# A hybrid encoder trunk on one core: the gated-delta stage woven from three generators, with TensorE's order written out

## The chip, the cores and the metric

One core of one Trainium2 chip runs the whole program. The metric is the device time of one execution in microseconds (us); the time of a kernel is the median of its runs.

## The reference

Two layers act on 768 tokens (one sequence of 512, one of 256; width 1024). The change lies in the first layer, in two of its parallel branches:

```
z = h @ w_in
# gated delta rule, 8 heads, chunks of tokens, forward and backward
qkv  = silu(centred_depthwise_conv(z_qkv, gdn_conv_w))        # width 5
q, k = l2_normalize(q) * 128**-0.5, l2_normalize(k)
g    = cumsum(log decay within a chunk);  decay = exp(g_i - g_j), lower part
a    = strict_lower((beta k) k^T * decay)
t_inv = inverse(I + a);  u = t_inv (beta v);  w = t_inv (beta k exp(g))
per chunk, in sequence: v_new = u - w S
                        o     = (q exp(g)) S + (q k^T * decay) v_new
                        S     = S * exp(g_last) + (k exp(g_last - g))^T v_new
y_b  = rms_norm(o_fwd + o_bwd) * silu(g_gdn)
# long convolution: its projections, short convolutions (width 3) and gates
uc = centred_depthwise_conv(z_hy, hy_conv_w) + hy_conv_b;  x0, x1, v = split(uc)
y_a = x0 * bidir_long_conv(v * x1) * silu(g_hy)
```

## The kernel before

The program is written with a tile framework: Python emits instructions, each engine gets its own queue, the framework places the semaphores. Unless told otherwise, a list scheduler orders each engine's queue: among what is ready by its own reckoning, the earliest in program order goes first; weight loads (`wload`) are moved 400 instructions ahead. On the chip each queue runs in that order.

**Projections.** `proj` multiplies one 128-column slice of the weights with all 768 tokens: 8 slices of the contraction, each with three products (high*high, high*low, low*high) over 512 and 256 columns, so 6 matmuls for each slice and 48 for a projection. The result takes one of two PSUM tiles `pp`. A weight slice comes by a DMA of SP's queue (L247), is rounded on ACT (L240), and its low part is made on POOL (L241). In the stage there are 64 projections: for each of 8 heads q, k, v and a gate (`gdn_proj`), for each of 8 channel groups four of the long convolution (`hy_proj`). Behind each come a convolution (`conv`: one ACT pass, L448, then on DVE, L455, eight multiply-adds for the delta rule's, four for the other's) or a gate (`silu2`, L327 on ACT, L328 on DVE).

**A head's front** (`gdn_front`, `gdn_inv`): transposes, norms, the masks `E` (ACT and POOL, L481), the products `A` and `Pm` (L554, L558); then the *gather*, by which the 32x32 diagonal blocks of `A` go through memory (bt to bd, L572; bd to B and W, L573 and L575); then the *inverse* of those blocks, 30 steps of two DVE instructions, each needing the one before (L589, L591); then the *scatter* of the blocks through memory into `TTN` (L592, L596, sixteen DMAs of L602).

**A head's back** (`gdn_back`): two levels of small matmuls that complete the inverse (L618 to L644; L618 is the first reader of `TTN`), the recurrence over chunks in four sequences (matmuls L667 and L668 on the state, L678 with the inverse, L686 and L688), then the norm and the output (`out`, L705 to L719).

The order of the program text is a string at the top:

```
ORDER = "F0 X0 F1 U0 B0 X1 F2 U1 B1 X2 F3 U2 B2 X3 F4 U3 B3 X4 F5 U4 B4 X5 F6 U5 B5 F7 X6 B6 U6 B7 X7 U7"
```

F is a head's projections, front and inverse, B a head's back, X and U are halves of a channel group's projections. So head i+1's projections and front stand before head i's back. The last head's output is emitted inside the next stage, the long convolution (`hyconv`), behind `hy_fwd(0)`.

Of the kernel before, what the change touches and what calls it, by code (L numbers as in the profile page):

```python
# [223 lines left out]
ORDER = "F0 X0 F1 U0 B0 X1 F2 U1 B1 X2 F3 U2 B2 X3 F4 U3 B3 X4 F5 U4 B4 X5 F6 U5 B5 F7 X6 B6 U6 B7 X7 U7"  # L224


class K:
# [34 lines left out]
    def proj(self, whl, m0=0):  # L262
        ps = self.pp.tile([128, 1024], F32, tag="pp", name="pp")[:, :T]
        for k in range(8):
            self.mm3(ps, whl, m0, self.hhi[k], self.hlo[k], k, k == 0, k == 7, ((0, 512), (512, 768)))
        return ps
# [177 lines left out]
    def conv(self, out, ps, taps, tile_ix, width, bias=None):  # L444
# [40 lines left out]
    def gdn_proj(self, p, h, n0):  # L485
        we = self.a["we"]
        kq = p.tile([128, 2, T], F32, tag="kq", name="kq", bufs=2)
        for i, nm in enumerate(("q", "k", "v")):
            w = self.wload(we[n0 + i], self.wp, 128)
            ps = self.proj(w)  # L490
            acc = p.tile([128, T], F32, tag="cv", name="cv", bufs=2)
            self.conv(acc, ps, V_GCW, 8 * i + h, 5)
            if nm == "v":
                vT = p.tile([128, T], F32, tag="vt", name="vT")
                dst = vT
# [4 lines left out]
        ps = self.proj(w)  # L500
        sg = p.tile([128, T], F32, tag="sg", name="sg", bufs=2)
        self.silu2(p, sg, ps)
        return kq, vT, sg

    def gdn_front(self, p, h, E, kq, vT, sg):
# [71 lines left out]
        return dict(kq=kq, sg=sg, kt=kt, nv=nv, rs=rs, ed=ed, A=A, Pm=Pm)  # L577

    def gdn_inv(self, p, h):
# [6 lines left out]
        for m in range(1, 31):  # L586
# [4 lines left out]
            nc.vector.tensor_tensor(out=W[:, :m, m + 1:], in0=W[:, :m, m + 1:], in1=tmp, op=ALU.add)  # L591
        nc.scalar.activation(out=B, in_=W.rearrange("p a b -> p b a"), func=AF.Copy)  # L592
# [11 lines left out]
    def gdn_back(self, p, h, kq, sg, kt, nv, rs, ed, A, Pm):  # L604
# [33 lines left out]
        nc.vector.tensor_scalar_mul(x, tv(ps, 64), -1.0)  # L638
        ps = self.bank()
# [3 lines left out]
        for d, eq, lq in hf:  # L643
            nc.scalar.activation(out=tt[d][eq, :, lq], in_=tv(ps, 64)[eq], func=AF.Copy)  # L644
        yield
# [11 lines left out]
        for step in range(4):  # L657
            for si, (d, seq) in enumerate(seqs):
                if step >= len(seq):
                    continue  # L660
                t = seq[step]
                ts = slice(128 * t, 128 * t + 128)
                if step == 0:
                    v1 = nv[:, t, :]
                else:
                    ps = self.bank()
                    mm(ps[:, :128], kq[:, 0, ts], S[si])  # L667
                    mm(ps[:, 128:256], kq[:, 1, ts], S[si])  # L668
                    v1 = p.tile([128, 128], F32, tag="v1", name="v1", bufs=3)
                    nc.vector.scalar_tensor_tensor(out=v1, in0=ps[:, :128], scalar=self.gneg[:, d, t, h:h + 1], in1=nv[:, t, :], op0=ALU.mult, op1=ALU.add)  # L670
                    eg = self.gex[:, 3 * d, t, h:h + 1]
                    if t not in seen:
                        nc.scalar.activation(out=o[:, t, :], in_=ps[:, 128:256], func=AF.Copy, scale=eg)
                        seen.add(t)
                    else:
                        nc.vector.scalar_tensor_tensor(out=o[:, t, :], in0=ps[:, 128:256], scalar=eg, in1=o[:, t, :], op0=ALU.mult, op1=ALU.add)
                ps = self.bank()
                mm(ps[:, :128], TTN[:, d, t, 0:128], v1)  # L678
                w = p.tile([128, 128], F32, tag="wv", name="wv", bufs=2)
                nc.vector.tensor_copy(w, ps[:, :128])  # L680
                last = step == len(seq) - 1
                if not last:
                    w2 = p.tile([128, 128], F32, tag="w2", name="w2", bufs=2)
                    nc.scalar.activation(out=w2, in_=ps[:, :128], func=AF.Copy, scale=ed[:, d, t:t + 1])
                ps = self.bank()
                mm(ps[:, :128], Pm[:, d, t, :], w)  # L686
                if not last:
                    mm(ps[:, 128:256], kt[:, t, :], w2)  # L688
# [12 lines left out]
                yield  # L701

# [9 lines left out]
        y = sg  # L712
        for t0, n in ((0, 4), (4, 2)):
# [4 lines left out]
            nc.vector.scalar_tensor_tensor(out=y[:, cs], in0=pt[:, :128 * n], scalar=self.vec(V_GN), in1=sg[:, cs], op0=ALU.mult, op1=ALU.mult)  # L718
        nc.scalar.dma_start(out=self.y[8 + h], in_=y)  # L719


    def hy_proj(self, p, c, n0, halves=(0, 1)):
        nc = self.nc

        def part(i):
            w = self.wload(self.a["we"][n0 + i], self.wp, 128)
            ps = self.proj(w)
            t = p.tile([128, T], F32, tag="hy", name="hy", bufs=2)
            if i < 3:
                self.conv(t, ps, V_HCW, 8 * i + c, 3, bias=self.vec(V_HCB + 8 * i + c))  # L730
            else:
                self.silu2(p, t, ps)
            return t
        for i, j, dst in [((1, 2, self.ud[c]), (0, 3, self.xd[c]))[x] for x in halves]:
            t0, t1 = part(i), part(j)
            nc.gpsimd.tensor_tensor(out=t1, in0=t1, in1=t0, op=ALU.mult)
            nc.scalar.dma_start(out=dst, in_=t1)

# [611 lines left out]
def trunk(tc, a, outs, dbg=None):  # L1350
    nc = tc.nc
    dbg = dbg or {}
    with ExitStack() as ctx:
# [24 lines left out]
        with ExitStack() as gd:  # L1378
# [32 lines left out]
            def front(i):  # L1411
                if i > 0:
# [151 lines left out]
```

## Time and profile before

| what | value |
|---|---|
| median of 3 runs | 2365.88 us (2364.73 to 2366.44) |
| the profiled execution | 2362.44 us, of which the span from first to last instruction is 2360.7 us |
| TensorE (PE) busy over the span | 2213.2 us (94%) |
| VectorE (DVE) / ScalarE (ACT) / GpSimd (POOL) busy | 1414.8 / 896.5 / 433.9 us |
| mean granted clock of TensorE | 0.974 of full speed |
| the stage of the change | 222.2 to 1044.2 us of the span |

Busy time counts instructions at work; a share of the span is a mean over stages with different limits, so the stage is looked at by itself.

### The profile page before, as it was taken

The numbers are of one execution on the slowest core, as the hardware profiler recorded it, in microseconds if no ns is written. First come the engines' busy times: TensorE is split into PE (matmuls) and PEld (weight loads), VectorE is DVE, ScalarE is ACT, GpSimd is POOL, SyncE is SP. The second block draws the span as 40 slices with busy tenths as digits, with TensorE's granted clock in tenths as the row PEclk, the third lists the DMA queues.
The fourth block names the chain that finished last, engine by engine and source line by source line (L and its number), as shares of the span: only waits on it lengthen the run. The fifth ranks groups of instructions, "written<-read, shape, count | busy, mean of one in ns | idle before, by whom it ended". The sixth has DMA issues, their size and how long they took to land. (4 is left out here: it accounts for less than half of the span.)

```text
span 2360.7 us, 35185 instructions
## 1 busy us (share of the span) xinstructions
PE 2213.2 (94%) x13648; PEld 1855.1 (79%) x13648; DVE 1414.8 (60%) x3236; ACT 896.5 (38%) x1888; POOL 433.9 (18%) x303
## 2 busy tenths in 40 slices
PE   8999898889999998889999979999999999999897
PEld 6788776777878887777778858988888877778785
DVE  6775387785776867758651264236555577664414
ACT  6333544435345344322142352122222344443423
POOL 2344242223233231223300140000000000000002
PEclk9999999999999998999999989999999999999898
DMA  7442223222223222246362342111111211111613
GB/s 247 138 158 96 73 84 78 82 82 73 78 73 90 78 62 60 67 165 222 113 197 62 102 135 90 54 56 58 52 46 43 77 50 50 40 62 46 203 63 107
DMA packets 122705, 218.98 MB, mean 93 GB/s; under 512 B 49592, under 2 KB 62297, under 8 KB 122282
## 3 DMA queue, kind: packets, MB, share of 16 engines
q1 hardware_dynamic: 102746, 171.86, 23.9%
q10 hardware_dynamic: 19568, 44.04, 5.0%
q8 instruction: 107, 1.75, 0.3%
q0 software_dynamic: 224, 0.83, 0.1%
q14 instruction: 60, 0.49, 0.1%
HBM read 174.43 MB, written 42.25 MB: 92 GB/s over the span
## 5 line engine op out<-in xcount | busy, mean ns | idle before, releaser
L256 PE MATMUL pp<-hhi,w 128*128 128x512 f32 (+1 forms) x2032 | 558.5, 348 | 20.5 <-DVE cv L455 9.6
L258 PE MATMUL pp<-hlo,w 128*128 128x512 f32 (+1 forms) x2032 | 553.6, 347 | 0.0
L260 PE MATMUL pp<-hhi,w 128*128 128x512 f32 (+1 forms) x2032 | 545.9, 344 | 0.0
L256 PEld LDWEIGHTS pp<-hhi,w 128*128 128x128 f32 (+1 forms) x2032 | 321.2, 190 | 68.3 <-issue 17.2
L258 PEld LDWEIGHTS pp<-hlo,w 128*128 128x128 f32 (+1 forms) x2032 | 319.4, 190 | 47.9 <-issue 6.6
L260 PEld LDWEIGHTS pp<-hhi,w 128*128 128x128 f32 (+1 forms) x2032 | 318.0, 189 | 44.8 <-issue 2.7
L1013 PE MATMUL pp<-yh,wo 128*128 128x256 f32 (+1 forms) x1152 | 274.1, 348 | 17.3 <-DVE wo L241 9.0
L240 ACT ACTIVATE w<-wr 128x1024 fp32r<-128x1024 f32 x155 | 163.3, 1053 | 296.6 <-PE pp L260 247.3
L241 POOL TENSOR_TENSOR w<-wr,w 128x1024 fp32r<-128x1024 f32 (+1 forms) x65 | 155.3, 2389 | 462.5 <-ACT w L240 305.4
L1013 PEld LDWEIGHTS pp<-yh,wo 128*128 128x128 f32 x1152 | 191.5, 195 | 48.8 <-ACT yh L240 11.5
L241 DVE TENSOR_TENSOR w<-wr,w 128x1024 fp32r<-128x1024 f32 x90 | 113.6, 1263 | 140.3 <-ACT w L240 140.1
L241 DVE TENSOR_TENSOR wo<-wor,wo 128x640 fp32r<-128x640 f32 (+1 forms) x76 | 62.0, 817 | 191.5 <-ACT wo L240 191.4
L1013 PE MATMUL pp<-yl,wo 128*128 128x512 f32 (+1 forms) x576 | 170.2, 349 | 0.2
L241 POOL TENSOR_TENSOR xk<-raw,xk 128x512 fp32r<-128x512 f32 x8 | 10.8, 1356 | 751.7 <-ACT xk L240 751.7
L455 DVE SCALAR_TENSOR_TENSOR cv<-pp,vecs,cv 128x510 f32<-128x510 f32 (+1 forms) x192 | 107.4, 605 | 24.7 <-ACT cv L448 24.7
L1013 PEld LDWEIGHTS pp<-yl,wo 128*128 128x128 f32 x576 | 100.1, 194 | 17.3 <-DVE yl L241 1.9
L240 ACT ACTIVATE wo<-wor 128x640 fp32r<-128x640 f32 (+1 forms) x76 | 52.0, 686 | 159.1 <-PE pp L1013 146.4
L589 DVE TENSOR_TENSOR Bt<-W,B 48x30 f32<-48x30 f32 (+14 forms) x240 | 98.5, 410 | 4.2 <-DMA B<-bd 2.5
L591 DVE TENSOR_TENSOR W<-W,Bt 48x30 f32<-48x30 f32 (+14 forms) x240 | 97.9, 408 | 1.8
L1022 POOL TENSOR_TENSOR oacc<-oacc,osq 128x768 f32<-128x768 f32 (+2 forms) x15 | 24.0, 1601 | 279.6 <-ACT osq L1018 279.6
L455 DVE SCALAR_TENSOR_TENSOR hy<-pp,vecs,hy 128x511 f32<-128x511 f32 x96 | 55.6, 606 | 30.6 <-ACT hy L448 30.2
L686 PE MATMUL pb<-wv,P 128*128 128x128 f32 x192 | 42.4, 303 | 20.9 <-DVE wv L680 20.9
(322 smaller groups left out, 3736.4 us busy)
## 6 DMA issues: line engine op xcount, KB each, us to landing
wr<-we SPq DMA_DIRECT2D x72, 512.0 KB, 3.5
wr<-wog SPq DMA_DIRECT2D x30, 512.0 KB, 3.6
wor<-weo SPq DMA_DIRECT2D x40, 320.0 KB, 3.2
wr<-wqk SPq DMA_DIRECT2D x24, 512.0 KB, 3.3
wor<-woo SPq DMA_DIRECT2D x36, 256.0 KB, 3.0
yr<-ye SPq DMA_DIRECT2D x20, 384.0 KB, 3.9
dec<-dec ACTq DMA_DIRECT2D x8, 768.0 KB, 4.3
fd<-F ACTq DMA_DIRECT2D x8, 768.0 KB, 3.5
```

Of the source, the lines that this page charges most:

```text
L240: nc.scalar.activation(out=hi, in_=src, func=AF.Copy)
L241: (lo_eng or self.lo_eng or nc.vector).tensor_tensor(out=lo, in0=src, in1=hi.bitcast(F32), op=ALU.subtract)
L256: mm(ps[:, s:e], wh, rhs_hi[:, s:e], start=first, stop=False)
L258: mm(ps[:, s:e], wh, rhs_lo[:, s:e], start=False, stop=False)
L260: mm(ps[:, s:e], wl, rhs_hi[:, s:e], start=False, stop=last)
L455: nc.vector.scalar_tensor_tensor(out=out[:, lo:hi], in0=ps[:, lo + s:hi + s], scalar=self.vec(taps + 24 * j + tile_ix), in1=out[:, lo:hi], ...
L589: nc.vector.tensor_tensor(out=tmp, in0=W[:, :m, m:m + 1].to_broadcast([48, m, n]), in1=B[:, m:m + 1, m + 1:].to_broadcast([48, m, n]), op= ...
L591: nc.vector.tensor_tensor(out=W[:, :m, m + 1:], in0=W[:, :m, m + 1:], in1=tmp, op=ALU.add)
L686: mm(ps[:, :128], Pm[:, d, t, :], w)
L1013: mm(ps[:, s:e], w[:, wi, j, :], y[order[i], g], start=i == 0 and x == 0, stop=i == nk - 1 and x == 2)
L1022: nc.gpsimd.tensor_tensor(out=acc[:, s:e], in0=acc[:, s:e], in1=sq[:, s:e], op=ALU.add)
```

## The change

The stage becomes three generators that are advanced in turns. A *piece* is six matmuls of a projection (one slice of the contraction). For every piece of `big` (all projections: per head four of the delta rule and then 24 pieces, three projections, of the long convolution) the loop advances the pending convolutions and gates (`k.post`) by four steps, the recurrences (`sb`) by one and the fronts (`sf`) by one. Inside this block TensorE's queue is not scheduled: it is in program order. The other engines are scheduled as before. A head's front is followed by ten empty pieces before its back may start; a front may start when the head two before it is done. The last head's output is now emitted inside the block. In the recurrence the sequences of a step are emitted side by side (all L667 and L668, then all L678, then all L686 and L688). `kq` has three buffers instead of two, `v1`, `wv` and `w2` four.

In steps of one piece, a front has 4 for the transposes of k and q, 2 for those of v, 6 empty ones, 3 for the products (L554), 30 for the inverse and the 10 empty ones behind it; the gather's instructions stand at the inverse's first step, the scatter's behind its last. A back has 9 for the two levels, then 8, 12, 9 and 9 for the recurrence's four steps (step 1 has four sequences, the last two steps have two), 4 empty ones and 2 for the output's transposes. `hy_proj` is cut into pieces and posts in the same way as `gdn_proj`.

```diff
-ORDER = "F0 X0 F1 U0 B0 X1 F2 U1 B1 ..."
+    def proj_g(self, whl):
+        ps = self.pp.tile([128, 1024], F32, tag="pp", name="pp")[:, :T]
+        for k in range(8):
+            self.mm3(ps, whl, 0, self.hhi[k], self.hlo[k], k, k == 0, k == 7, ((0, 512), (512, 768)))
+            if k < 7:
+                yield
         return ps
-    def conv(self, out, ps, taps, tile_ix, width, bias=None):
+    def conv_g(self, out, ps, taps, tile_ix, width, bias=None):
...
                 nc.vector.scalar_tensor_tensor(
...
+                yield
-    def gdn_proj(self, p, h, n0):
+    def gdn_proj(self, p, h, n0, settled):
...
+        for i, nm in enumerate(("q", "k", "v")):
+            w = self.wload(we[n0 + i], self.wp, 128)
+            ps = yield from self.proj_g(w)
+            self.post.append(post(i, nm, ps))
+            yield
         w = self.wload(we[n0 + 3], self.wp, 128)
+        ps = yield from self.proj_g(w)
+        settled()
+        self.post.append(post_g(ps))
+        yield
+        return st
@@ gdn_front
+            yield
+        for _ in range(6):
+            yield
...
@@ gdn_inv
             nc.vector.tensor_tensor(out=W[:, :m, m + 1:], in0=W[:, :m, m + 1:], in1=tmp, op=ALU.add)
+            yield
...
@@ gdn_back
-            for si, (d, seq) in enumerate(seqs):
...
+            live = [(si, d, seq[step], step == len(seq) - 1) for si, (d, seq) in enumerate(seqs) if step < len(seq)]
+            v1s, ws = {}, {}
+            for si, d, t, last in live:
...
+                yield
+            if 0 < len(live) < 4 and step:
+                yield
+            for si, d, t, last in live:
...
+                ws[si] = w, w2
+                yield
+            if len(live) < 4:
+                yield
+            for si, d, t, last in live:
+                w, w2 = ws[si]
...
                 yield
+            if len(live) < 4:
+                yield
...
+        for _ in range(4):
+            yield
...
-    def hy_proj(self, p, c, n0, halves=(0, 1)):
+    def hy_proj(self, p, c, n0):
...
-            for ch in ORDER.split():
...
+            def small_front():
+                for i in range(8):
+                    while i not in fronts or i - 2 in st:
+                        yield
+                    E, q = fronts.pop(i)
+                    sg = q.pop("sg")
+                    st[i] = dict((yield from k.gdn_front(p, i, E, **q)), sg=sg)
+                    yield from k.gdn_inv(p, i)
+                    for _ in range(10):
+                        yield
+                    backs.append(i)
+            def small_back():
+                for i in range(8):
+                    while i not in backs:
+                        yield
+                    yield from k.gdn_back(p, i, **st[i])
+                    del st[i]
+            def big():
+                hys = chain(*(k.hy_proj(p, c, 32 + 4 * c) for c in range(8)))
+                for i in range(8):
+                    if i > 0:
+                        E = k.gdn_decay(p, i)
+                    q = yield from k.gdn_proj(p, i, 4 * i, lambda: settled(i - 2))
+                    if i == 0:
+                        k.gdn_gates(p)
+                        E = k.gdn_decay(p, 0)
+                    while "sg" not in q:
+                        run(k.post)
+                    fronts[i] = E, q
+                    for _ in range(24):
+                        next(hys)
+                        yield
+                yield from hys
...
+            with tc.manual_schedule(engines={mybir.EngineType.PE}):
+                for _ in big():
+                    for _ in range(4):
+                        run(k.post)
+                    next(sb, None)
+                    next(sf, None)
+                while k.post:
+                    run(k.post)
+                for _ in sb:
+                    next(sf, None)
...
                     f = k.hy_fwd(p2, 0)
-                out(7)
```

## Rows read from the trace of the kernel before

**Rows 1.** Busy time by stretch: length, then PE, PEld, DVE, ACT, POOL, clock, DMA.

```profile
222.20:1044.20 822.00, 750.04 (x5560) 640.15 (x5559) 572.74 (x1608) 360.56 (x909) 230.53 (x108) 0.97 0.27 79
662.40:758.60 96.20, 89.71 (x688) 77.24 (x687) 70.24 (x200) 44.63 (x112) 28.85 (x13) 1.00 0.28 79
674.60:709.70 35.10, 31.81 (x210) 28.00 (x209) 34.00 (x107) 11.45 (x33) 6.85 (x3) 1.00 0.13 43
```

**Rows 2.** Waits of PE in the stage: us in total, times, longest.

```profile
PE pb L686 <- DVE wv L680: 20.9, 18, 2.5
...
PE pb L426 <- DVE g L423: 4.2, 1, 4.2
...
PE pb L332 <- ACT zT L404: 1.9, 1, 1.9
```

**Rows 3.** Timeline of PE: start, us, engine, line, operation, tiles, shape.

```profile
660.19 0.51 PE L256 MATMUL pp<-hhi,w 128*128 128x512 f32 x2
...
661.25 0.51 PE L256 MATMUL pp<-hhi,w 128*128 128x512 f32 x2
...
678.78 0.39 PE L667 MATMUL pb<-S,kq 128*128 128x128 f32 x2
679.00 0.39 PE L668 MATMUL pb<-S,kq 128*128 128x128 f32 x2
```

**Rows 4.** Timeline of DVE: end of a gather's input, an inverse's first and last.

```profile
655.93 1.08 DVE L558 TENSOR_TENSOR A<-pb,A 128x256 f32<-128x256 f32 x3 [1.51 <-POOL A L539]
...
674.62 0.14 DVE L589 TENSOR_TENSOR Bt<-W,B 48x30 f32<-48x30 f32 x1
...
682.13 2.52 DVE L591 TENSOR_TENSOR W<-W,Bt 48x210 f32<-48x210 f32 x1
...
709.51 0.20 DVE L591 TENSOR_TENSOR W<-W,Bt 48x30 f32<-48x30 f32 x1
```

**Rows 5.** Timeline of SP's queue, the DMAs of gather and scatter.

```profile
660.51 2.00 SPq L572 DMA_DIRECT2D bd<-bt  x4
...
668.90 0.33 SPq L573 DMA_DIRECT2D B<-bd  x1
...
718.69 3.02 SPq L602 DMA_DIRECT2D TTN<-wd  x6
```

**Rows 6.** DMA issues, 500 to 900 us: count, KB each, median us to landing.

```profile
TTN<-wd SPq DMA_DIRECT2D x64, 24.0 KB, 2.4
...
bd<-bt SPq DMA_DIRECT2D x16, 48.0 KB, 2.5
```

**Rows 7.** Groups of DVE in one inverse, 674.6 to 709.7: busy us, mean ns | idle.

```profile
L591 DVE TENSOR_TENSOR W<-W,Bt 48x30 f32<-48x30 f32 (+14 forms) x30 | 13.0, 433 | 0.3
L589 DVE TENSOR_TENSOR Bt<-W,B 48x30 f32<-48x30 f32 (+14 forms) x30 | 11.3, 378 | 0.2
...
L455 DVE SCALAR_TENSOR_TENSOR hy<-pp,vecs,hy 128x511 f32<-128x511 f32 (+1 forms) x4 | 2.4, 599 | 0.0
```

**Rows 8.** Groups of DVE in the stretch behind it, 709.8 to 758.6.

```profile
L455 DVE SCALAR_TENSOR_TENSOR cv<-pp,vecs,cv 128x510 f32<-128x510 f32 (+3 forms) x24 | 13.3, 608 | 1.9 <-ACT cv L448 1.9
...
L328 DVE SCALAR_TENSOR_TENSOR kq<-th,cv 128x768 f32<-128x768 f32 x2 | 1.9, 954 | 1.0 <-ACT th L327 1.0
```

**Rows 9.** Timeline of POOL: two masks, and a weight's low part.

```profile
658.22 3.98 POOL L481 TENSOR_TENSOR E<-E,cm 128x768 f32<-128x768 f32 x2
...
682.02 2.40 POOL L241 TENSOR_TENSOR w<-wr,w 128x1024 fp32r<-128x1024 f32 x1 [11.10 <-ACT w L240]
```

**Rows 10.** Timeline of PE where the stage ends.

```profile
1039.95 0.82 PE L332 MATMUL pb<-cm,eu 128*128 128x128 f32 x6
...
1043.96 1.06 PE L826 MATMUL pb<-Rf,f 128*128 128x128 f32 x8
1046.44 0.63 PE L332 MATMUL pb<-cm,o 128*128 128x128 f32 x4 [1.42 <-DVE o L711]
...
1051.03 1.22 PE L905 MATMUL pp<-g,Y 128*128 128x257 f32 x2 [2.91 <-POOL Y L879]
```

More of the change, by code (lines that the diff above doesn't have):

```diff
@@ L483, in gdn_decay, with post @@
         return E
-    def gdn_proj(self, p, h, n0):
+    def gdn_proj(self, p, h, n0, settled):
         we = self.a["we"]
[L487 to L490, printed above, removed]
+        st = {}
+        kq = st["kq"] = p.tile([128, 2, T], F32, tag="kq", name="kq", bufs=3)
+        def post(i, nm, ps):
             acc = p.tile([128, T], F32, tag="cv", name="cv", bufs=2)
-            self.conv(acc, ps, V_GCW, 8 * i + h, 5)
+            yield from self.conv_g(acc, ps, V_GCW, 8 * i + h, 5)
             if nm == "v":
-                vT = p.tile([128, T], F32, tag="vt", name="vT")
-                dst = vT
+                dst = st["vT"] = p.tile([128, T], F32, tag="vt", name="vT")
             else:
@@ new lines, in gdn_back @@
+                    v1s[si] = nv[:, t, :]
+                    continue
+                ps = self.bank()
+                mm(ps[:, :128], kq[:, 0, ts], S[si])
+                mm(ps[:, 128:256], kq[:, 1, ts], S[si])
+                v1 = v1s[si] = p.tile([128, 128], F32, tag="v1", name="v1", bufs=4)
+                nc.vector.scalar_tensor_tensor(out=v1, in0=ps[:, :128], scalar=self.gneg[:, d, t, h:h + 1], in1=nv[:, t, :], op0=ALU.mult, op1=ALU.add)
+                eg = self.gex[:, 3 * d, t, h:h + 1]
@@ L677, in gdn_back @@
+                if t not in seen:
+                    nc.scalar.activation(out=o[:, t, :], in_=ps[:, 128:256], func=AF.Copy, scale=eg)
+                    seen.add(t)
+                else:
+                    nc.vector.scalar_tensor_tensor(out=o[:, t, :], in0=ps[:, 128:256], scalar=eg, in1=o[:, t, :], op0=ALU.mult, op1=ALU.add)
+                yield
+            if 0 < len(live) < 4 and step:
+                yield
+            for si, d, t, last in live:
                 ps = self.bank()
-                mm(ps[:, :128], TTN[:, d, t, 0:128], v1)
@@ L679, in gdn_back @@
-                w = p.tile([128, 128], F32, tag="wv", name="wv", bufs=2)
+                mm(ps[:, :128], TTN[:, d, t, 0:128], v1s[si])
+                w = p.tile([128, 128], F32, tag="wv", name="wv", bufs=4)
                 nc.vector.tensor_copy(w, ps[:, :128])
-                last = step == len(seq) - 1
+                w2 = None
                 if not last:
-                    w2 = p.tile([128, 128], F32, tag="w2", name="w2", bufs=2)
+                    w2 = p.tile([128, 128], F32, tag="w2", name="w2", bufs=4)
@@ L684, in gdn_back @@
                     nc.scalar.activation(out=w2, in_=ps[:, :128], func=AF.Copy, scale=ed[:, d, t:t + 1])
+                ws[si] = w, w2
+                yield
+            if len(live) < 4:
+                yield
+            for si, d, t, last in live:
+                w, w2 = ws[si]
                 ps = self.bank()
+                if not last:
+                    mm(ps[:, 128:256], kt[:, t, :], w2)
                 mm(ps[:, :128], Pm[:, d, t, :], w)
                 if not last:
-                    mm(ps[:, 128:256], kt[:, t, :], w2)
@@ L701, in gdn_back @@
                 yield
+            if len(live) < 4:
+                yield
         self.mark("g.out%d" % h)
@@ L712, in gdn_back @@
         y = sg
+        for _ in range(4):
+            yield
         for t0, n in ((0, 4), (4, 2)):
@@ L718, in gdn_back, with post, gate @@
             nc.vector.scalar_tensor_tensor(out=y[:, cs], in0=pt[:, :128 * n], scalar=self.vec(V_GN), in1=sg[:, cs], op0=ALU.mult, op1=ALU.mult)
+            yield
         nc.scalar.dma_start(out=self.y[8 + h], in_=y)
-    def hy_proj(self, p, c, n0, halves=(0, 1)):
+    def hy_proj(self, p, c, n0):
         nc = self.nc
[L725 to L728, printed above, removed]
+        def post(i, ps, t):
             if i < 3:
-                self.conv(t, ps, V_HCW, 8 * i + c, 3, bias=self.vec(V_HCB + 8 * i + c))
+                yield from self.conv_g(t, ps, V_HCW, 8 * i + c, 3, bias=self.vec(V_HCB + 8 * i + c))
             else:
                 self.silu2(p, t, ps)
-            return t
-        for i, j, dst in [((1, 2, self.ud[c]), (0, 3, self.xd[c]))[x] for x in halves]:
-            t0, t1 = part(i), part(j)
+                yield
+        def gate(t0, t1, dst):
             nc.gpsimd.tensor_tensor(out=t1, in0=t1, in1=t0, op=ALU.mult)
             nc.scalar.dma_start(out=dst, in_=t1)
+            yield
+        for i, j, dst in ((0, 3, self.xd[c]), (1, 2, self.ud[c])):
+            ts = []
+            for x in (i, j):
+                ps = yield from self.proj_g(self.wload(self.a["we"][n0 + x], self.wp, 128))
+                ts.append(p.tile([128, T], F32, tag="hy", name="hy", bufs=2))
+                self.post.append(post(x, ps, ts[-1]))
+                if x == j:
+                    self.post.append(gate(*ts, dst))
+                yield
     def sine(self, p, out, ps, b, freq, n):
@@ L1427, in back @@
-            def back(i):
-                st["o", i] = k.gdn_back(p, i, **st.pop(i))
-                for _ in range(13):
-                    next(st["o", i])
-            def out(i):
-                for _ in st["o", i]:
-                    pass
-            run = {"F": front, "B": back, "U": lambda c: hy(c, (0,)), "X": lambda c: hy(c, (1,))}
-            for ch in ORDER.split():
-                i = int(ch[1])
-                run[ch[0]](i)
-                if ch[0] == "B" and i < 7:
-                    out(i)
+            k.post = []
@@ new lines, in run, with settled @@
+            def run(q):
+                if q and next(q[0], k) is k:
+                    q.pop(0)
+            sf, sb = small_front(), small_back()
+            def settled(i):
+                while i in st:
+                    next(sb)
+            with tc.manual_schedule(engines={mybir.EngineType.PE}):
[8 more added lines that the diff above has]
+                    next(sf, None)
```

54 lines of the change are left out of this document (17 added, 37 removed).

## The prediction

> **What bounds the kernel now.** I read first the busy time by stretch, then who waits for whom on TensorE, then the timelines of one head. The stage of the change lasts 822.0 us, and PE works in 750.0 of them [rows 1]: 72.0 us of idle time are all that an order of TensorE without gaps could win. Of these, 6.1 (4.2 and 1.9) lie in the gates, which stay as they are [rows 2]; 65.9 can go. The largest share, 20.9 us, is the recurrence waiting for a copy on DVE [rows 2], up to 2.5 us at a time. From one head's first use of its inverse to the next (662.4 to 758.6) 96.2 us pass; PE idles for 6.5 and DVE is busy for 70.2 [rows 1]. DVE's load isn't even: during an inverse it works in 34.0 of 35.1 us [rows 1], and only one convolution of the light kind and a gate stand beside inverse and recurrence there [rows 7]. So PE is the bound on average, and DVE is in that third of a head. The inverse itself holds nobody up before: this one, begun at 674.62 [rows 4], is first used at 758.6, the border of that stretch in rows 1, 34 us after its scatter landed (below).
>
> **The change, part by part.** I count pieces from the first one of a head's q projection. A head takes 32 + 24 = 56 pieces. Its front begins at piece 32, its products stand at 44 to 46, the gather at 47, the inverse at 47 to 76, the ten empty pieces at 77 to 86, its back begins at 88. At 56 the next head's projections begin, so its q and k convolutions (emitted from pieces 64 and 72 on) now stand inside this inverse, and so do steps 1 to 3 of the recurrence of the head before. Since PE's queue is fixed, the first L618 at piece 88 holds every projection behind it until the scatter has landed. The question is whether 41 pieces (47 to 87) last as long as the chain from products to scatter.
>
> *The pieces.* Six matmuls take 661.25 - 660.19 = 1.06 us [rows 3]; 41 take 43.5. Between them stand 40 pairs of small matmuls of the recurrence (4 of step 0, 18, 10 and 8 of steps 1 to 3) and six transposes at half a pair; a pair takes 679.00 - 678.78 = 0.22 us [rows 3], together 9.5. A head before has 96.2 - 6.5 = 89.7 us of work; by such prices I reach about 87.5, so 1.5 us more are due in 41 of 64 pieces. Sum: 54.5 us.
>
> *The chain.* (a) The last product takes 1.1 us [rows 4]. (b) The gather: from 655.93 + 1.08 = 657.0 to the inverse's first instruction at 674.62 [rows 4] 17.6 us pass. Of these, 3.9 were a queue: the blocks were written by 660.51 + 2.00 + 2.5 = 665.0, and read only at 668.90, behind a weight load in SP's queue [rows 5, 6]. That load's place is the scheduler's again, so the price is 13.7 to 17.6; I take the middle, 15.6. (c) The inverse: 709.71 - 674.62 = 35.1 us [rows 4] with what ran beside it. Its own 60 instructions take 13.0 + 11.3 = 24.3 [rows 7]. After the change the light convolution and the gate beside it go (3.3 us: 2.4 [rows 7] and a gate of 0.95 [rows 8]), and about 4 of the recurrence fall into the gather's wait. What comes is two convolutions of the heavy kind with their gates, 13.3/3 + 0.95 = 5.4 us each [rows 8], and about 1 of a light one. 35.1 - 3.3 - 4 + 10.8 + 1 = 39.6, of which I take 39, as the k convolution may end behind the inverse's last steps. Bounds: 24.3, if DVE does nothing else until it is done, and 45, with the lock below. (d) The scatter: from 709.71 to the last issue at 718.69 + 3.02 = 721.71 [rows 4, 5], and 2.4 to its landing [rows 6]: 14.4; the code is unchanged and SP issues in the same way. Sum: 1.1 + 15.6 + 39 + 14.4 = 70.1 us; bounds 1.1 + 13.7 + 24.3 + 14.4 = 53.5 and 1.1 + 17.6 + 45 + 14.4 = 78.1.
>
> *The new wait.* 70.1 - 54.5 = 15.6 us for each of heads 1 to 6: 94. Head 0 has no recurrence beside it: its chain is 1.1 + 15.6 + 36 + 14.4 = 67.1, its pieces 43.5 + 1 = 44.5, the wait 22.6. Head 7 has only light convolutions beside it, 39 - 10.8 + 4 = 32, so 63.1 - 54.5 = 8.6. Sum: 125 us. Where in the head PE waits (at a late copy of the recurrence, or at L618) doesn't change it. Queued behind are all projections, so nothing fills it; bounds by the chain's 53.5 and 78.1: 9 and 190.
>
> *A lock.* At 682.02 POOL began a weight's low part of 2.40 us; the inverse's next step on DVE began at 682.13 and took 2.52, where the mean of its line is 0.43 [rows 4, 7, 9]. Three POOL operations did so in this inverse, and they are in (c). The two masks of the next head, 3.98 us [rows 9], stood outside the inverse and move into it (piece 56); I price that between 0 and 4 and take 0, since a convolution or a copy may stand in front on DVE. [...]
>
> *What goes.* The 65.9 us of waits in the old places [rows 1, 2]. Side by side, the sequences leave three to four pieces, over 3 us, between a result and its reader, where the longest of this kind of wait was 2.5 [rows 2]. At least those 20.9 should go; I take all, for a wait that stays elsewhere in a head is hidden in the chain's.
>
> *The end.* The last output's transposes (1046.44) come behind a chain on DVE and ACT as before. But `hy_fwd(0)`'s matmuls, 1039.95 to 1043.96 + 1.06 [rows 10], which filled that wait, now stand behind them in program order: 5.1 us; 0 if they are still scheduled ahead, 10 if L905's wait (1051.03) comes free of cover too.
>
> *At nothing:* the more buffers; the yields themselves; the projections, which are the same 64; switching between large and small matmuls, as often as before and in the dense price. If a convolution is late, the covering PSUM tile is one projection, about 10 us.
>
> *Sum.* 2362.4 (the profiled execution) - 65.9 + 125 + 5 = 2426.5. The median of the runs shown is 3.4 above that execution: **2430 us**, 2.7% slower.
>
> **The rivals.** *The inverse is done first* (faster). The scheduler may find the inverse's steps ready before the convolutions and put them in front. Then (c) is its own 24.3 and about 4 of the recurrence, the chain 59.4, the wait 4.9 a head: 6 x 4.9 + 11.4 + 4.9 = 46; 2365.9 - 65.9 + 46 + 5 = 2351. With the gather at 13.7 and a tail of 0 it is 2331; I put the case at 2340. For it: these steps are ready as soon as W is loaded, and stand earlier in the text than the q convolution up to piece 63. Against: before, the same rule left one inverse stretched from 24.3 to 35.1 [rows 7]. It decides at waits of 61 us in all, 7.6 a head: an inverse of 31 us. *The lock in full* (slower yet): 4 us more in each of 8 chains: 2430 + 32 = 2462. For it speaks the one shown; against, that DVE has work from PSUM to put between. *Nothing happens*: the scheduler's order had few gaps, and new waits take just the place of old ones (a chain of about 62 us): 2366.
>
> **How the numbers follow.** My forecast (chain over 63 us, lock as before) has 0.47, the lock 0.13, the inverse first 0.33, no change 0.07: slower 0.47 + 0.13 = 0.60, faster 0.33, same 0.07. A difference within 0.2% (4.7 us) is what a measurement can't tell from none. The forecast's own range is 2385 to 2470 (chains of 65 to 75 us). The range for 8 in 10 has cases of both signs in it: 2315, just below the faster rival with its better ends, to 2475, above the lock.
>
> **What would show it.** Right: PE idle in the stage above 100 us; waits of L618, or of the recurrence's L678 and L686, behind DVE or the TTN load, over 10 us a head, and a granted clock that falls after them; DVE nearly full between gather and scatter; an inverse of some 39 us; L618 in steps of about 97 us from head to head (89.7 - 8.5 for a projection less + 15.6) although only 7 projections lie between. Wrong: PE idle under 60 us; an inverse of under 31 us with q's multiply-adds behind it; TTN landing before PE reaches L618. The tail is right if no L905 starts within 5 us of the output's transposes. If the stage's waits fall as I say and the time falls too, the error is in the price of dense pieces.

## The result

The changed kernel takes 2437.3 us (median of 4 runs, 2432.4 to 2441.0) where the kernel before takes 2366.2: 1.0306 of it, interval 1.0292 to 1.0320, slower by 71 us. The forecast was 2430.

### The profile page after: what moved, and what is told of

Read it like the earlier page. It is cut to its first block, busy times and chain, and to the rows that moved or that the text cites. A ratio compares the mean times of both kernels' runs of the same rounds, so it can differ in the third digit from the quotient of the medians.

```text
span 2437.0 us, 35142 instructions
## 1 busy us (share of the span) xinstructions
PE 2226.3 (91%) x13648; PEld 1877.1 (77%) x13648; DVE 1416.4 (58%) x3236; ACT 893.6 (37%) x1888; POOL 431.3 (18%) x303
## 5 line engine op out<-in xcount | busy, mean ns | idle before, releaser
L255 PE MATMUL pp<-hhi,w 128*128 128x512 f32 (+1 forms) x2032 | 581.1, 365 | 6.8 <-DVE cv L463 4.3
L257 PE MATMUL pp<-hlo,w 128*128 128x512 f32 (+1 forms) x2032 | 546.8, 348 | 0.0
L259 PE MATMUL pp<-hhi,w 128*128 128x512 f32 (+1 forms) x2032 | 541.0, 346 | 0.0
L259 PEld LDWEIGHTS pp<-hhi,w 128*128 128x128 f32 (+1 forms) x2032 | 320.9, 193 | 49.5 <-issue 2.7
L255 PEld LDWEIGHTS pp<-hhi,w 128*128 128x128 f32 (+1 forms) x2032 | 324.9, 195 | 43.5 <-issue 9.9
L463 DVE SCALAR_TENSOR_TENSOR cv<-pp,vecs,cv 128x510 f32<-128x510 f32 (+1 forms) x192 | 110.4, 603 | 17.2 <-ACT cv L456 17.2
L615 DVE TENSOR_TENSOR Bt<-W,B 48x30 f32<-48x30 f32 (+14 forms) x240 | 95.5, 398 | 6.6 <-issue 3.8
L617 DVE TENSOR_TENSOR W<-W,Bt 48x30 f32<-48x30 f32 (+14 forms) x240 | 96.7, 403 | 2.8
L335 ACT ACTIVATE th<-cv 128x768 f32<-128x768 f32 x24 | 20.2, 844 | 146.6 <-DVE cv L463 146.6
```

What stands on the lines that cost most here:

```text
L255: mm(ps[:, s:e], wh, rhs_hi[:, s:e], start=first, stop=False)
L257: mm(ps[:, s:e], wh, rhs_lo[:, s:e], start=False, stop=False)
L259: mm(ps[:, s:e], wl, rhs_hi[:, s:e], start=False, stop=last)
L463: nc.vector.scalar_tensor_tensor(out=out[:, lo:hi], in0=ps[:, lo + s:hi + s], scalar=self.vec(taps + 24 * j + tile_ix), in1=out[:, lo:hi], ...
L615: nc.vector.tensor_tensor(out=tmp, in0=W[:, :m, m:m + 1].to_broadcast([48, m, n]), in1=B[:, m:m + 1, m + 1:].to_broadcast([48, m, n]), op= ...
```

## The profile after

Lines have moved: the inverse's two steps are now L615 and L617, the first reader of TTN is L645 (L618 before), the recurrence's matmuls are L716 (L678), L731 and L732 (L688, L686), its copies L718 on DVE and L722 on ACT.

To compare nearly equal work, the stage is taken from 222.2 us to the end of the last output's transpose (after the change 15 matmuls of `hy_fwd(0)`, some 2 us, fall behind that border). Busy time by stretch, before (columns as in [rows 1]):

```profile
222.20:1048.10 825.90, 751.94 (x5571) 641.40 (x5569) 575.97 (x1617) 360.56 (x909) 231.66 (x111) 0.97 0.27 79
```

And after: the stage, then the stretches of heads 0, 1, 3 and 7 from the last product's matmul to the first reader of TTN, then one inverse:

```profile
222.20:1122.00 899.80, 765.20 (x5556) 664.97 (x5555) 577.15 (x1614) 358.86 (x910) 228.01 (x111) 0.92 0.25 74
...
295.10:368.30 73.20, 46.83 (x253) 40.20 (x251) 47.43 (x106) 23.92 (x41) 21.95 (x10) 0.85 0.27 76
398.40:467.20 68.80, 58.35 (x338) 51.32 (x337) 56.35 (x154) 27.13 (x58) 18.01 (x9) 0.90 0.27 80
...
596.00:665.60 69.60, 57.12 (x336) 50.01 (x334) 57.70 (x158) 27.50 (x58) 18.21 (x9) 0.95 0.27 79
...
994.60:1059.10 64.50, 57.76 (x338) 50.38 (x336) 51.18 (x139) 19.42 (x40) 15.73 (x7) 0.95 0.27 79
...
614.40:653.50 39.10, 27.52 (x151) 23.80 (x150) 37.22 (x104) 9.13 (x24) 6.28 (x3) 0.91 0.14 50
```

The stage is 73.9 us longer: 60.6 of idle time (134.6 less 74.0) and 13.3 of busy time (765.20 less 751.94), at a granted clock of 0.92 where it was 0.97. The part behind it (span less 1122.0, and less 1048.1) is 2.4 longer. From last product to first reader a middle head takes about 69 us, and PE idles in 10 to 12.5 of them; DVE works in 37.2 of the inverse's 39.1 us. Its groups on DVE, as [rows 7] (beside them the gates' 1.9 us and the recurrence's 6.7):

```profile
L615 DVE TENSOR_TENSOR Bt<-W,B 48x30 f32<-48x30 f32 (+14 forms) x30 | 13.1, 435 | 0.3
L617 DVE TENSOR_TENSOR W<-W,Bt 48x30 f32<-48x30 f32 (+14 forms) x30 | 11.7, 390 | 0.3
L463 DVE SCALAR_TENSOR_TENSOR cv<-pp,vecs,cv 128x510 f32<-128x510 f32 (+3 forms) x16 | 9.6, 601 | 0.0
```

Who waits for whom on PE in the stage (us in total, times, longest):

```profile
PE pb L731 <- ACT w L722: 37.5, 10, 5.7
PE pb L645 <- DMA TTN<-wd: 28.3, 15, 19.6
PE pb L732 <- DVE wv L718: 26.7, 7, 4.5
PE pb L716 <- ACT TTN L678: 17.2, 7, 2.5
...
PE pb L434 <- DVE g L431: 4.2, 1, 4.2
```

The 20.9 us of [rows 2] for the recurrence's copies, at most 2.5 at a time, have become 64, up to 5.7 at a time; the wait for TTN is 19.6 in head 0, but under 1 at a time elsewhere. Where a long one comes from stands in the timelines (start, us, engine, line). DVE first, in the inverse of head 3:

```profile
624.78 0.28 DVE L718 COPY wv<-pb 128x128 f32<-128x128 f32 x1
624.98 0.36 DVE L617 TENSOR_TENSOR W<-W,Bt 48x210 f32<-48x210 f32 x1
625.26 0.73 DVE L463 SCALAR_TENSOR_TENSOR cv<-pp,vecs,cv 128x510 f32<-128x510 f32 x1
625.92 0.37 DVE L615 TENSOR_TENSOR Bt<-W,B 48x220 f32<-48x220 f32 x1
...
631.21 0.47 DVE L463 SCALAR_TENSOR_TENSOR cv<-pp,vecs,cv 128x254 f32<-128x254 f32 x1
...
631.92 0.27 DVE L718 COPY wv<-pb 128x128 f32<-128x128 f32 x1
```

ACT, in the same time:

```profile
631.77 0.84 ACT L335 ACTIVATE th<-cv 128x768 f32<-128x768 f32 x1 [6.31 <-DVE cv L463]
632.52 0.35 ACT L722 ACTIVATE w<-pb,ed 128x128 f32<-128x128 f32 x1
```

And PE:

```profile
626.76 0.52 PE L259 MATMUL pp<-hhi,w 128*128 128x512 f32 x2
632.92 0.80 PE L731 MATMUL pb<-w,kt 128*128 128x128 f32 x2 [5.64 <-ACT w L722]
...
633.80 0.99 PE L255 MATMUL pp<-hhi,w 128*128 128x512 f32 x2
...
635.84 0.51 PE L255 MATMUL pp<-hhi,w 128*128 128x512 f32 x2
...
665.64 0.24 PE L645 MATMUL pb<-TTN,A 32*32 32x32 f32 x2 [0.94 <-DMA TTN<-wd]
```

The q convolution's eight multiply-adds alternate with the inverse's steps from 625.26 to 631.7. The second sequence's copy stands behind them on DVE, and on ACT behind a tanh that waits for them. PE, whose next instruction needs that copy, does nothing for 5.64 us with projections in its queue, and then runs at a granted clock of 0.50 until 635.8: 0.99 us for what takes 0.51 right after, at 1.00.

## The experiments

One table for all. Step: mean of the six from the second to the eighth head's first reader, with 41 to 43 projections in each run's six. Inverse, chain (last product's matmul to the last block of TTN landed) and lag (last landing to first reader; about -3 means that PE begins as the first block lands): medians of heads 1 to 6.

| run | us | ratio (interval) | step | inverse | chain | lag |
|---|---|---|---|---|---|---|
| before | 2366.2 | | 89.5 | 35.1 | 73.1 | 34 |
| after | 2437.3 | 1.0306 (1.0292 to 1.0320) | 98.6 | 39.6 | 72.0 | -3 |
| e1 | 2402.8 | 1.0145 (1.0119 to 1.0171) | 94.0 | 44.6 | 77.2 | -2 |
| e2 | 2492.9 | 1.0533 (1.0514 to 1.0552) | 106.6 | 25.3 | 55.5 | 23 |
| e3 | 2433.3 | 1.0287 (1.0266 to 1.0308) | 100.6 | 37.8 | 69.0 | 25 |
| e4 | 2399.3 | 1.0138 (1.0120 to 1.0157) | 95.6 | | none | |
| e5 | 2447.5 | 1.0344 (1.0323 to 1.0366) | 99.6 | 43.7 | 76.3 | -3 |
| e6 | 2403.0 | 1.0156 (1.0140 to 1.0172) | 96.0 | | none | |
| e7 | 2407.3 | 1.0172 (1.0153 to 1.0190) | 97.9 | 49.6 | 83.0 | 7 |
| e8 | 2405.5 | 1.0165 (1.0148 to 1.0183) | 97.2 | 48.4 | 82.1 | 7 |
| e9 | 2374.7 | 1.0052 (1.0032 to 1.0073) | 90.6 | 32.4 | 62.8 | -3 |
| e10 | 2411.8 | 1.0205 (1.0190 to 1.0221) | 95.8 | 37.6 | 72.4 | 17 |
| e11 | 2427.7 | 1.0269 (1.0252 to 1.0285) | 98.2 | 40.0 | 70.8 | -3 |
| e12 | 2366.5 | 1.0006 (0.9996 to 1.0017) | 90.5 | 38.3 | 71.5 | -0.5 |

**e1**, PE scheduled:

```diff
-            with tc.manual_schedule(engines={mybir.EngineType.PE}):
+            if True:
```

> The changed kernel with the fixing of TensorE's order taken away and nothing else: the program text stays woven, and the scheduler again chooses what PE does next. Chain theory (the 41 pieces between a head's products and the first reader of its inverse are shorter than the 72 us that gather, inverse and scatter take, and a fixed queue lets nothing pass the waiting matmul): projections move ahead of the waits, PE idle in the stage falls from 130 to about 70 us and the time to some 2370 us (2355 to 2385). Crowding theory (what PE waits for are the recurrence's copies on DVE and ACT, late because convolutions and inverse share DVE in the same third of a head): the copies stay late but projections pass them too, so about the same, 2370. Rival that the weave of the text itself is the loss, with the order only its carrier: 2420 or more.

2402.8: above what both theories gave and below the rival's 2420. In this text, fixing the order costs 35 us of the 71 (2437.3 less 2402.8); the other 37 are there with PE scheduled too. PE's largest waits are now those of projections:

```profile
PE pp L255 <- DVE cv L463: 33.7, 13, 5.5
PE pp L255 <- DVE sg L336: 18.5, 6, 4.7
```

**e2**, the inverse first on DVE:

```diff
...
-            yield
+        self.hold = last.ins
...
+        for _ in range(30):
+            yield
...
-                if q and next(q[0], k) is k:
+                    with tc.issue_after(k.hold) if k.hold else nullcontext():
+                        done = next(q[0], k) is k
```

> The changed kernel with the inverse's thirty steps emitted at once (thirty empty pieces behind them, so all places stay) and the convolutions that are emitted after them put behind its last step in DVE's order. PE's order is that of the changed kernel. Chain theory: the inverse falls from 39 to about 28 us, the chain from 72 to 61, the step from head to head from 98.7 to about 88, the time by about 7 x 10 to some 2365 us (2350 to 2385). Crowding theory: the same copies now stand behind inverse and convolutions together, so the waits stay where they are and the time stays within 10 us of 2437.

Both missed: the inverse fell to 25.3 us and TTN landed 23 us ahead of its reader, and the kernel became slower yet. DVE's timeline (gather, inverse, convolution):

```profile
511.35 0.63 DVE L595 TENSOR_TENSOR bt<-bt,nmask 128x384 f32<-128x384 f32 x1
...
523.07 0.20 DVE L615 TENSOR_TENSOR Bt<-W,B 48x30 f32<-48x30 f32 x1
...
548.28 2.17 DVE L463 SCALAR_TENSOR_TENSOR hy<-pp,vecs,hy 128x511 f32<-128x511 f32 x4
```

and PE's:

```profile
550.60 0.98 PE L255 MATMUL pp<-hhi,w 128*128 128x512 f32 x2 [21.01 <-DVE hy L463]
```

A convolution behind the inverse also stands behind the gather that the inverse waits for, some 37 us in all (511 to 548), and a projection's PSUM tile covers about 10 (an estimate: eight pieces of 1.06 us and what stands between them). So the edit tests more than the inverse's length; it shows that a chain shortened at this cost to the convolutions gains nothing, not what a short chain is worth by itself.

**e3**, the back ten pieces later, and **e4**, TTN loaded from a constant ahead of the inverse:

```diff
                     while i not in backs:
                         yield
+                    for _ in range(10):
+                        yield
```

```diff
...
+                    nc.sync.dma_start(out=v[32 * b:32 * b + 32, :, c0:c0 + 32], in_=self.wz[w, b, d].rearrange("t j i -> j t i"))
         tmpf = p.tile([48, 256], F32, tag="Bt", name="Bt")
...
-                    nc.sync.dma_start(out=v[32 * b:32 * b + 32, :, c0:c0 + 32], in_=wd[w, b, d].rearrange("t j i -> j t i"))
```

> The changed kernel with each head's back begun ten pieces later (an empty stretch of ten pieces in the backs' own stream, so that the fronts keep their places). Chain theory: ten pieces more, 10.6 us, stand between products and first reader in every head, waits fall by up to 10 us a head and by 10 of head 0's 19.6; the last back ends ten pieces later without cover, +5 to +10: some 2370 us (2360 to 2385). Crowding theory: the recurrence moves ten pieces out of the thirty in which the next inverse runs, so about a third of the 81 us of waits for its copies goes, with the same cost at the end: about 2415 us.

> The changed kernel with the loads of TTN taken from a constant in DRAM and issued ahead of the inverse, so that no reader waits for gather, inverse or scatter; the inverse's blocks are still computed and written but not used (that part of the result is left out). DVE's load and PE's order stay. Chain theory: without the chain PE waits for almost nothing but the copies' few tenths of a us, idle in the stage falls from 130 to about 30 us, the step from head to head to about 86 us, the time to about 2345 us (2335 to 2365). Crowding theory: only the 28 us of waits for TTN itself go, the 81 us of waits for the recurrence's copies stay: about 2410 us.

e3 gave 2433.3: TTN was there 25 us early, and the step did not fall (100.6). But the edit does more than move the back. At the end of a head's gate projection `settled` runs the back of the head two before to its end. Counted from the first piece of its own head, that back is done at piece 141 in the changed kernel, ahead of the 144 at which `settled` asks; in e3 it would be done at 151. So in heads 0 to 5 the output's six transposes (L340) come with no piece between them and the last L732, where the changed kernel has six pieces (counted in both traces), and PE waits 7.0 us each time, 42 of 49.8 us in all:

```profile
655.34 0.38 PE L732 MATMUL pb<-wv,P 128*128 128x128 f32 x2
662.75 1.54 PE L340 MATMUL pb<-cm,o 128*128 128x128 f32 x6 [7.03 <-DVE o L758]
```

So e3 doesn't test the chain's cover alone: less these 7.0 its step would be some 94, an estimate that holds only if nothing took their place. Its other waits are L716 behind its own input from DVE (32.4) and the ACT copies (26.8).

e4 gave 2399.3, near the crowding theory's 2410 and far from the chain theory's 2345. Its waits of PE:

```profile
PE pb L735 <- ACT w L726: 36.5, 10, 5.6
PE pb L736 <- DVE wv L722: 26.6, 7, 4.5
PE pb L720 <- ACT TTN L682: 18.2, 7, 3.3
```

These are the same three waits at the same price. Of the 38 us won, 18.3 are head 0 (its first reader at 350.0 and not 368.3), and 3.0 a step (98.6 less 95.6) most of the rest. So the chain is one limit of a step, 98.6 us, and something on DVE and ACT is another, 95.6, just under it.

**e5 to e8.** The copies first (e5), with e4's loads (e6), with e3's later back (e7), and that with the output's normalisation first too (e8). One of the copies, as the others:

```diff
...
+                with self.tc.high_priority(offset=300):
-                nc.vector.tensor_copy(w, ps[:, :128])
+                    nc.vector.tensor_copy(w, ps[:, :128])
...
```

> The changed kernel with the recurrence's and the inverse levels' own operations on DVE and ACT (the copies between its matmuls) given a higher priority in the scheduler, so that they stand ahead of the convolutions on those queues; PE's order and all places stay. Two-bounds theory (after the run without the chain: the copies' waits and the chain are two limits of nearly the same height, 98.7 us a head by both and 95.9 by the copies alone): the 81 us of waits for the copies nearly go, but PE then reaches the first reader of the inverse up to 12 us earlier in a head and waits there instead, because the chain of 72 us is no shorter: waits for TTN rise from 28 to some 80 to 100 us, time 2415 to 2435. Copies-alone theory: the 81 us go and little comes back, 2360 us.

> The run before together with the loads of TTN from a constant, ahead of the inverse (the inverse's result is left unused). Two-bounds theory: with both limits gone PE idles under 40 us in the stage, a step from head to head takes 84 to 87 us, time 2325 to 2350. If fixing the order costs by itself, through other late results that neither limit holds: 2380 or more, as without the chain alone.

> The copies first, and each head's back begun ten pieces later, with the whole result computed. Two-bounds theory: the chain gets 10.6 us more cover, the copies stand ahead of the convolutions, so both waits go but for head 0 (some 9 us) and the output's transposes, whose DVE chain kept PE for 49.8 us when the back was later: 2370 to 2390 us; without those 49.8, 2340. Chain as the only bound: about 2360. Copies as the only bound, no better than the copies first alone.

> The run before with the output's normalisation on DVE given the same priority. Two-bounds theory: the waits of the output's transposes for it, up to 7 us a head, go as well: 2335 to 2355 us, below the kernel before. If it only pushes convolutions back until PE waits for a free PSUM tile, the time stays at that of the run before.

e5, waits of PE:

```profile
PE pb L340 <- DVE o L773: 55.1, 8, 9.2
PE pp L255 <- DVE cv L463: 44.3, 14, 5.6
PE pb L645 <- DMA TTN<-wd: 35.2, 13, 19.0
...
PE pb L741 <- ACT w L732: 2.5, 4, 0.9
```

The copies' waits did go, from 64 us to under 4, and I was wrong about what comes back: not mainly the wait for TTN (28.3 to 35.2), but the output's normalisation and the convolutions, until projections wait for their PSUM tile. The chain grew with them (inverse 43.7). e6 shows that the copies aren't the second limit by themselves: without the chain and with the copies first I expected 84 to 87 us a step, and got 96.0; its two largest waits are the same:

```profile
PE pb L340 <- DVE o L777: 54.0, 8, 9.2
PE pp L255 <- DVE cv L463: 43.8, 13, 5.3
```

In e5 and e6 PE's fixed queue met what now stood behind the copies. e7 missed too: 2407.3, over its 2370 to 2390, with TTN there 7 us early. But it and e8 have e3's later back, and with it the output without a piece in front of it in heads 0 to 5: 7.8 to 9.3 us each, 50 of e7's 59.7 and 52 of e8's 61.0 at L340. So that e8, with the output first on DVE, stays at e7's time doesn't show what such an order is worth. The waits of projections for the convolutions are there in both (40.4 and 43.2).

**e9 to e12.** e9 leaves out the outer taps of q's and k's convolutions; e10 to e12 move the gate projection and with it the front behind the head's 24 pieces of the long convolution, "Hyena" below (e10 with e3's later back, e12 with e1's edit):

```diff
-            yield from self.conv_g(acc, ps, V_GCW, 8 * i + h, 5)
+            yield from self.conv_g(acc, ps, V_GCW, 8 * i + h, 5 if nm == "v" else 1)
```

```diff
...
                     for _ in range(24):
                         next(hys)
                         yield
+                    E = k.gdn_decay(p, i)
+                    yield from q.pop("last")()
+                    while "sg" not in q:
+                        run(k.post)
+                    fronts[i] = E, q
```

> The changed kernel with one tap instead of five in the q and k convolutions: their sixteen multiply-adds a head on DVE, 9.6 us, are left out, so the output is of a different convolution; PE's work and order stay. Full-DVE theory (in the third of a head that holds inverse, two heavy convolutions, recurrence and output chain, DVE has more work than PE's pieces last, and every order of DVE makes something late): the waits for the recurrence's copies behind the convolutions (L731 and L732, 64 us) fall under 15, the inverse to about 30 us, the step from head to head from 98.7 to about 88, time 2355 (2340 to 2375). Rival that a fixed order of PE meets late results wherever they come from: the step stays over 94 and the time over 2400.

> The whole computation with PE's order fixed, but a head's gate projection and front stand behind its 24 Hyena pieces (24 pieces later), so that the inverse runs beside Hyena's light convolutions and not beside q's and k's; the back is begun ten pieces later. Full-DVE theory: the step from head to head falls to 86 to 91 us; the last head's back, 34 pieces later, runs almost without projections beside it, which costs 30 to 45 us: time 2385 to 2430. Rival that the fixed order costs wherever the work stands: steps of 97 or more and 2460 us.

> The same shift of the front without the later back. Here the chain has the 41 pieces of the changed kernel again, and an inverse beside light convolutions of some 35 us. If the chain is a bound by itself once DVE isn't full: 1.1 + 16 + 35 + 14.4 = 66.5 against 54.5, so PE waits about 10 us a head for TTN, steps of about 93, time 2400 to 2440. If only DVE's fullness held PE: steps of 86 to 90 as with the later back, and a shorter end: 2370 to 2400.

> The same shift of the front with the order of PE left to the scheduler. Full-DVE theory (the weave of the text puts the inverse beside the heavy convolutions, and that is why the woven text was 36 us over the kernel before even with PE scheduled): steps of 87 to 90 against 94, the end some 15 to 20 us longer, time 2370 to 2395. If the weave costs for other reasons: steps of 94 again and 2415 or more.

e9: 2374.7, at the upper end of what I gave it. 9.6 us less of DVE operations a head took 8.0 off the step and 9 off the chain, and the copies' waits nearly went:

```profile
PE pb L645 <- DMA TTN<-wd: 22.2, 11, 11.0
PE pb L340 <- DVE o L758: 19.7, 7, 4.7
PE pb L716 <- ACT TTN L678: 17.3, 7, 2.5
...
PE pb L731 <- ACT w L722: 4.8, 5, 2.1
PE pb L732 <- DVE wv L718: 4.4, 7, 0.9
```

e10 (2411.8) and e11 (2427.7) lie in their ranges, but the steps missed: beside light convolutions I expected an inverse of 35 us, with steps of 86 to 91 (later back) and about 93. The inverse took 37.6 and 40.0, and the steps stayed at 95.8 and 98.2; in an inverse of e10 (531 to 569 us) DVE spends 26.6 us on its own steps, 4.5 on light convolutions and a gate, and 8.3 on the recurrence, which I had left out. In e10 the step again holds 7.0 us of an output without pieces in front (heads 0 to 5); less these it would be about 89, inside the 86 to 91, an estimate as for e3. e11 has its six pieces, and its lag is -3: there the chain bounds it again. e12 is the surprise, and below my range: with the same shifted text and PE scheduled, 2366.5, no different from the kernel before. Its largest waits:

```profile
PE pb L340 <- DVE o L761: 27.5, 8, 4.7
PE pb L735 <- DVE wv L721: 10.8, 9, 2.3
PE pb L734 <- ACT w L725: 6.0, 7, 2.0
```

With e11's text, fixing the order costs 61 us (2427.7 less 2366.5). And the woven text's 37 us in e1 go when gate projection, front and inverse are moved away from the heavy convolutions (e12): of e1's waits of projections, 33.7 and 18.5, 4.3 and 3.9 are left. Which of the three moved parts does it wasn't separated. No version was faster than the kernel before.

## Why the prediction was right or wrong

**Sign and size: right**, 7 us short and inside the forecast's own 2385 to 2470. The size is partly luck, as the terms show, in us:

| term | foreseen | measured |
|---|---|---|
| PE idle, last product to first reader, head 0 | 22.6 | 26.4 |
| the same, heads 1 to 6 | 94 | 64.5 |
| the same, head 7 | 8.6 | 6.7 |
| PE idle outside these stretches, without the gates | 0 | 31 |
| PE busy time of the stage | 0 | +13.3 |
| behind the stage | +5 | +2.4 |

The idle times are those of the eight stretches (such as 68.80 less 58.35); they sum to 97.6, and 134.6 less 97.6 less 6.1 for the gates leaves the 31. Idle time grew by 60.6 where I had 125 - 65.9 = 59: two terms were off by about 30 each and cancelled by luck. All terms come to 64 foreseen and 76 measured between the profiled executions; the medians lie 71 apart.

Of the signs that I named, idle time, inverse, DVE's load and steps came as written. The largest wait, though, is L731 (L688 before) behind a copy on ACT, 37.5 us, and L645 itself waits for little behind head 0.

**The chain was right.** Foreseen 1.1 + 15.6 + 39 + 14.4 = 70.1, and 96.8 a step; measured 72.0 (gather 16.3, inverse 39.6, scatter 15.0), and 98.6. In the fixed order with the lag at -3, PE stands at the reader when TTN lands, and without the chain the step falls by 3.0 (e4): the chain is the higher limit, by that little. Step less median chain is 26.6 us (foreseen 26.7), 27.8 in e9 and 27.4 in e11, at chains from 63 to 72; in e5 it is 23. That the 26.6 fits is luck again: from a reader to the next head's last product 30 us pass and not 26.7, but PE begins about 3 us before TTN's last block has landed, and head 7's stretch is shorter.

**The pieces.** I had 54.5 us of PE work in 41 pieces; PE was busy for 57.1 to 59.6 in heads 1 to 6, at a clock of 0.90 to 0.95. In the trace 6.3 to 11.6 us of this lie at a granted clock of 0.50; with half of that taken off, an estimate from 0.99 us for 0.51, 53.8 to 54.2 are left, so the pieces were priced rightly for a granted clock of 1.00. The missing term is the clock: I named its fall after waits as a sign and gave it no price. About 4 us more of busy time and 3 us by which PE begins ahead of the last block, against a chain 2 longer, make the idle time of heads 1 to 6 64.5 instead of 94. Over the stage the granted clock was 0.50 for 51 us before and 152 after, with PE busy in 37 and 107 of them: half of these 70 us more, some 35, is what the clock cost, an estimate from 0.99 us for 0.51. Of it 13.3 show in the busy time, since the other work took some 20 us less; at a granted clock of 1.00 the small matmuls start on average 55.5 ns behind each other where it was 62.3 (waits left out).

**What goes: wrong.** I took all 65.9, "for a wait that stays elsewhere in a head is hidden in the chain's". That holds for the recurrence's copies: "three to four pieces between a result and its reader" don't cover a copy behind a whole convolution, but 63 of its 64 us lie between products and reader, in place of the wait for TTN. It fails between a reader and the next head's products: PE passes there before the next chain can start, so a wait there lengthens the step in full. The 31 us lie there and behind head 7: 17.2 is the first L716 behind the copy that ends the inverse's levels (ACT, L678), which the side-by-side order does nothing for; 4.7 is the last output, 4.6 the later blocks of TTN, 4.2 the last head's recurrence. The levels' own wait before:

```profile
PE pb L636 <- DVE TTN L629: 8.6, 4, 2.3
```

So this term was worth about 35 and not 65.9. And I counted one limit only: without the chain the same waits are a limit of their own at 95.6 us a step (e4).

**The rivals.** *The inverse first* didn't come: the inverse took 39.6. Its price of 2340 wasn't tested by itself. e2's inverse of 25.3 us, under the 31 that were to decide, gave 2493, but with the convolutions behind the gather as well; e9's 32.4 gave 2375, with DVE relieved as well. The price counted the chain as the only limit, and e4 shows the second one. *The lock in full*: steps of the inverse over 1 us were 25 of 480 before (53.3 us in all) and 21 of 480 after (46.9), so the extra of 0 that I took was right, but not for the reason given. Each of these long steps, 25 and 21, lies beside a POOL operation, and of the POOL operations that began in an inverse 25 of 28 met one before and 17 of 19 after. What kept the extra at 0 is that the two masks didn't move into the inverse: on POOL they stand in the gather (L490 at 597.16 and 601.62 for the inverse of 614.4). One of the steps:

```profile
639.77 2.39 POOL L240 TENSOR_TENSOR w<-wr,w 128x1024 fp32r<-128x1024 f32 x1 [16.83 <-issue]
639.84 2.56 DVE L617 TENSOR_TENSOR W<-W,Bt 48x210 f32<-48x210 f32 x1
```

*Nothing happens* didn't come either: 3% slower, clear of the 0.2%.

**The end.** Behind it the time grew by 2.4 us, half of what I gave. The place was right: the output's transposes now wait, and `hy_fwd(0)`'s matmuls stand behind the first of them, the first L962 (L905 before) 6.6 us behind the last (1128.60 less 1122.0).

```profile
1118.45 1.33 PE L340 MATMUL pb<-cm,o 128*128 128x128 f32 x5 [4.68 <-DVE o L758]
...
1125.26 1.06 PE L883 MATMUL pb<-Rf,f 128*128 128x128 f32 x8
...
1128.60 1.14 PE L962 MATMUL pp<-g,Y 128*128 128x257 f32 x4 [1.85 <-POOL Y L936]
```

**Open.** What a fixed order would reach with both limits gone wasn't measured: e6 put the output and the convolutions behind, and the runs with a later back (e3, e7, e8, e10) lost the output's cover. What DVE's share in the second limit is, by itself, was not separated: e9 shortens the chain and empties DVE at once. Whether the order of PE alone would cost as much in the kernel before's own text wasn't tried. The more buffers and the side-by-side recurrence weren't tried alone either; e12 has both and takes as long as the kernel before.

## What to carry to other kernels

A fixed order on one engine is only as good as the order of the engines that feed it: those were still scheduled, and each late result stopped everything queued behind it (35 us in one text, 61 in another). When such a queue runs in a loop, ask of each wait whether the chain runs beside it or starts only behind it: the first kind is hidden, the second is paid in full. Before pricing a chain against its cover, look for a second limit of the same height in the same stretch: take the chain away and see what step is left. And where an engine is nearly full in a stretch, putting one of its results first only chose which reader waits (e5, e6); moving the inverse out of the stretch took the woven text's 37 us away where PE was scheduled (e12), and 10 where its order was fixed (e11). And an edit that delays one of several woven streams can run into a rule by which another waits for it: count what PE has between a result and its reader in the new trace before reading the time.

## What the runs showed of the hardware

The granted clock was 0.92 over the stage where it was 0.97, with 134.6 us of idle time where there were 74.0. After a wait of 5.64 us a pair of matmuls took 0.99 us for 0.51, at a granted clock of 0.50 until 635.8. In all it was 0.50 for 152 us of the stage and not 51, worth some 35 us of PE's time by the estimate above, beside 60.6 us more of idle time. From products to first reader, where TTN's landing set the end, PE was busy for about 58 us instead of 54 and idle for that much less: there the clock's price was hidden.

An inverse step on DVE that ran beside a POOL operation could take as long as that operation: 2.56 us beside one of 2.39, where the mean of its line in that inverse is 0.39. All 46 steps over 1 us, before and after, lie beside one. The convolutions' multiply-adds, which read PSUM, took 0.748 us inside a POOL operation and 0.735 without one (means on 128x510, after the change).
